# Making the context's modulation columns beside token blocks 2 and 3, and the context's tokens and states earlier in the first head pair

## The chip, the cores and the metric

The kernel runs on one core of a Trainium2 chip. The metric is the device time of one execution, in microseconds; the median of three runs is given. The engines are TensorE (PE in the profile), VectorE (DVE), ScalarE (ACT), GpSimd (POOL) and SyncE (SP, which issues most DMAs). Each engine carries out its own instructions in a fixed order and waits on semaphores for what other engines make.

## The reference

One layer of a hybrid diffusion backbone over 2048 tokens of width 1024, with 256 context tokens. What bears on the change is the modulated input of the context and the state that it leaves for the scans:

```python
mod_c = jax.nn.silu(c_ctx) @ w_mod[l] + b_mod[l]
csh1, csc1, cgt1, csh2, csc2, cgt2 = jnp.split(mod_c[None, None, :], 6, axis=-1)

uc = modulate(layer_norm(ctx), csh1, csc1)
fc, qc, kc, vc, gc = mixer_inputs(uc, w_in[l])
yc, st_f, st_b = bidirectional_retention(qc, kc, vc, lg_f, lg_b, state0, state0)

u = modulate(layer_norm(x), sh1, sc1)
f, q, k, v, g = mixer_inputs(u, w_in[l])
q = axial_rope(q, row_pos, col_pos)
k = axial_rope(k, row_pos, col_pos)
y, _, _ = bidirectional_retention(q, k, v, lg_f, lg_b, st_f, st_b)
mix = jnp.concatenate([fourier_mix(f), gated_group_norm(y, g)], axis=-1) @ w_out[l]
x = layer_norm(DEEPNORM_ALPHA * x + gt1 * mix, ln1_g[l], ln1_b[l])
```

Here `modulate(xn, shift, scale)` is `xn * (1 + scale) + shift`. The retention works in chunks of 128 tokens with one state per head and direction: each chunk adds to the state, decayed by the chunk's factor, and reads the state before it ("cross") and itself ("inner"). The latent tokens' scans start from the context's final states. A SwiGLU channel mixer follows.

## The kernel before, in words

Weights and activations are split into a high and a low f16 part, and every product of the large projections is three matmuls (lines 152 to 154, `mm3`). The 2048 tokens are four blocks of 512. The Tile scheduler sets the order of instructions on each engine from the program's text and its own timeline, so an instruction can stand far from where the text has it.

- *Blocks 0 and 1* are normalised and modulated together with the modulation's own columns: column block k (128 channels) of shift and scale is a product of `w_mod` with the conditioning vector, for the latent tokens (`smod[0]`) and, for k = 0 and 1 alone (`ON_PE = 2`), also for the context (`smod[1]`).
- *Blocks 2 and 3* follow in the loop `for b in range(2, NB)`: load four token tiles, two early projections (`early_mm`) of the first pair's q, k and v, normalise (line 229), and for each k four transposes (line 236), the f16 part on ScalarE (line 241), the f32 value on VectorE (line 246) and their difference on GpSimd (line 247). The Fourier group's projections and transforms come next, with more early projections: eight of sixteen chunks are projected when the pairs begin.
- *Three head pairs.* Each has a first pass (`first_pass`), which in every step projects a chunk and does rotation, turn (transposes), score and inner product of two ready ones, and then calls `side(s)` for work that is to lie beside it. In the first pair, `side1` starts one context column (`ctx_cols`) in each of the steps 0 to 5, the two context tiles (`ctx_tile`) in steps 5 and 6 and the context's keys and states (`pair.context()`) in step 8. Then `scans` carry the states from chunk to chunk on VectorE (`scan1`, line 684), and the second pass (`second_pass`) does gates (`gate`, SiLU at line 772), the cross products (line 784) and the normalised output. The modulation's columns of the later stages are summed in steps of the other pairs (`rest`).
- *A context column* (`ctx_cols`): `mod_sum` loads 1024 x 256 weights of `w_mod` in two tiles of 512 KB (line 559), sums them on VectorE with the vector's values, eight instructions of 128x256 (lines 561 and 563); two matmuls with a column of ones (line 572) add up the partitions; `mod_cols` (line 215) writes `smod[1][k]`. It yields after the sum, so that the matmuls come a step later.
- *A context tile* (`ctx_tile`): load (512 KB), normalise, eight transposes in two groups (line 586) and for each of them two activations of ScalarE (lines 241 and 244) and a subtraction.
- *The context's states* (`context`): two projections, keys (line 624), and four instructions that make the first state of each direction (lines 673 and 674).

All these weights and tiles go through three `raw` buffers of 512 KB, which are taken in the order of the program's text; a load waits until its buffer's last reader is done.

Of the kernel before, what the change touches and what calls it, by code (L numbers as in the profile page):

```python
# [12 lines left out]
ALU = mybir.AluOpType  # L13
PSUM = bass.MemoryType.PSUM

P = 128
D = 1024
KT = D // P
# [61 lines left out]
def layer_kernel(ctx: ExitStack, tc: tile.TileContext, a, out):  # L80
    nc = tc.nc
    V, S, G, T, Q = nc.vector, nc.scalar, nc.gpsimd, nc.tensor, nc.sync
    x_in = a["x"][0]
    ctx_in = a["ctx"][0]
    w_mod = a["w_mod"][0]
# [10 lines left out]
    def nm(s):  # L96
        uid[0] += 1
        return f"{s}_{uid[0]}"

    def mk(pool, shape, dt=F32, tag=None, bufs=1):  # L100
        return pool.tile(shape, dt, name=nm(tag), tag=tag, bufs=bufs)
# [8 lines left out]
    def const(shape, tag, dt=F32):  # L110
        return cp.tile(shape, dt, name=tag, tag=tag, bufs=1)


    pa = ctx.enter_context(tc.tile_pool(name="psum", bufs=1, space=PSUM))
# [13 lines left out]
    def raw_tile(shape=(P, 2, 512), dt=F32):  # L128
        return mk(wp, list(shape), dt, tag="raw", bufs=3)
# [6 lines left out]
    ones = const([P, 1], "ones")  # L136
# [57 lines left out]
    sil = const([P, 2, 8], "sil")  # L194
# [7 lines left out]
    def gemv(pool, raw, v, cols, tag):  # L202

        acc = mk(pool, [P, cols], tag=tag, bufs=2)
        V.tensor_scalar_mul(acc, raw[:, 0], sil[:, v, 0:1])
        for k in range(1, KT):
            V.scalar_tensor_tensor(acc, raw[:, k], sil[:, v, k : k + 1], acc, ALU.mult, ALU.add)
        return acc


    smod = [[const([P, 2], f"smod{v}_{k}") for k in range(KT)] for v in range(2)]
    smod2 = [const([P, 2], f"smod2_{k}") for k in range(KT)]

    def mod_cols(dst, pm, sub, k):
        V.scalar_tensor_tensor(dst, pm, SU, bmod[:, sub, k], ALU.mult, ALU.add)
# [15 lines left out]
    def u_part(pool, xs, hi, lo, s, k, tag, on_act):  # L231

        w = len(xs) * P
        pt = mk(pa, [P, 512], tag=tag, bufs=1)
        for i, xt in enumerate(xs):
            T.transpose(pt[:, i * P : (i + 1) * P], xt[:, k * P : (k + 1) * P], ident)
        u_split(pool, pt[:, :w], hi, lo, s, on_act)

    def u_split(pool, pt, hi, lo, s, on_act):
        w = pt.shape[1]  # L240
        S.activation(hi, pt, AF.Identity, scale=s[:, 1:2], bias=s[:, 0:1])
        u32 = mk(pool, [P, w], tag=f"u32_{w}", bufs=2)
        if on_act:
            S.activation(u32, pt, AF.Identity, scale=s[:, 1:2], bias=s[:, 0:1])
        else:
            V.tensor_scalar(u32, pt, s[:, 1:2], s[:, 0:1], ALU.mult, ALU.add)
        G.tensor_tensor(lo, u32, hi, ALU.subtract)
# [26 lines left out]
    def load_x(b):  # L274
        r = []
        for i in range(4):
            t = mk(sp, [P, D], tag="x", bufs=9)
            Q.dma_start(t, x_in[(b * 4 + i) * P : (b * 4 + i + 1) * P])
            r.append(t)
        return r  # L280

    ON_PE = 2
# [22 lines left out]
    q0, k0 = FW, FW + QKW  # L305
# [17 lines left out]
    for k in range(KT):  # L323
        while k and len(wms) < min(KT, k + 7):
            load_wm()
        pm = mk(pa, [P, 2, 2], tag="misc", bufs=2)
# [6 lines left out]
        else:  # L333
            acc = gemv(sp, wms[k].rearrange("p k i n -> p k (i n)"), 0, 2 * P, "macc")
# [24 lines left out]
    def early_mm(i):  # L359
# [4 lines left out]
            proj(ps, uhi[b][:, k, ts_], ulo[b][:, k, ts_], wq0[k], k)  # L364
        S.copy(early[i], ps)

    for b in range(2, NB):
        xs[b] = load_x(b)
        u_tiles(b)
        early_mm(2 * b - 4)  # L370
        for t in xs[b]:
            normalise(sp, t)
        early_mm(2 * b - 3)
        for k in range(KT):
            u_part(sp, xs[b], uhi[b][:, k], ulo[b][:, k], smod[0][k], k, ("tq", "zt")[k % 2], False)

    rope = ca.tile([P, NT, P], F32, name="rope", tag="rope", bufs=1)
    Q.dma_start(rope, a["rope"])
# [170 lines left out]

    gate_rows = [dram_tile([1, D], F32, f"gate{i}") for i in range(2)]  # L550


    def mod_sum(segs, v):

        r = []
        for k0 in range(0, KT, 4):
            raw = raw_tile((P, 4, 2, P))
            for i, c0 in enumerate(segs):
                Q.dma_start(raw[:, :, i], w_mod[k0 * P : (k0 + 4) * P, c0 : c0 + P].rearrange("(k p) n -> p k n", p=P))
            r.extend(raw[:, k].rearrange("p i n -> p (i n)") for k in range(4))  # L560
        V.tensor_scalar_mul(r[0], r[0], sil[:, v, 0:1])
        for k in range(1, KT):
            V.scalar_tensor_tensor(r[0], r[k], sil[:, v, k : k + 1], r[0], ALU.mult, ALU.add)
        return r[0]

    def ctx_cols(k):

        acc = mod_sum([i * D + k * P for i in range(2)], 1)
        yield
        pm = mk(pa, [P, 2], tag="zt", bufs=1)  # L570
        for i in range(2):
            T.matmul(pm[:, i : i + 1], acc[:, i * P : (i + 1) * P], ones, start=True, stop=True)
        mod_cols(smod[1][k], pm, 0, k)

    def ctx_tile(i):
        if not cu:
            cu.extend(up.tile([P, KT, CTX], F16, name=t, tag=t, bufs=1) for t in ("chi", "clo"))
        t = raw_tile((P, D))
        Q.dma_start(t, ctx_in[i * P : (i + 1) * P])
        normalise(rp, t)  # L580
        yield
        cs = slice(i * P, (i + 1) * P)
        for k0 in range(0, KT, 4):
            pt = mk(pa, [P, 4, P], tag="zt", bufs=1)
            for k in range(4):
                T.transpose(pt[:, k], t[:, (k0 + k) * P : (k0 + k + 1) * P], ident)
            for k in range(4):
                u_split(rp, pt[:, k], cu[0][:, k0 + k, cs], cu[1][:, k0 + k, cs], smod[1][k0 + k], True)
# [318 lines left out]
    def start(g):  # L907
        next(g)
        going.append(g)
# [10 lines left out]
    for p, pair in enumerate(pairs):  # L920
        wgu = pair.wg_units()

        def side1(s):
            go(s)
            if s is None:
                return
            if p == 0:
                n = KT - ON_PE
                if s < n:
                    start(ctx_cols(ON_PE + s))  # L930
                if s in (n - 1, n):
                    start(ctx_tile(s - n + 1))
                elif s == n + 2:
                    start(pair.context())
            elif s == 1:
                start(pair.context())
            if p and (p == 2 or s < 10) and rest:
                start(rest.pop(0)())
            if s >= (4 if p == 0 else 8) and wgu:
                wgu.pop(0)()  # L940

        nxt = pairs[p + 1].wq_units() if p + 1 < PAIRS else []

        def side2(s):
            go(s)
            if s is None:
                return
            if s >= 2 and s % 2 == 0 and nxt:
                nxt.pop(0)()
            elif p == PAIRS - 1 and s >= 3 and s % 2 and s < 11:  # L950
                wo_unit(0, s // 2 - 1, ws_tile)

        pair.first_pass(side1, early if p == 0 else ())
        pair.second_pass(orders[p][1], side2)
    es_r.close()
# [551 lines left out]
    for o, sb in TWO:  # L1507
        hq, last = h_next
        n = TWO.index((o, sb)) + 1
# [163 lines left out]
```

## Time and profile before

| | before |
|---|---|
| runs | 2156.97, 2154.32, 2148.89 us |
| median | 2154.32 us |
| profiled execution | 2151.64 us |
| its span | 2149.8 us |
| mean granted clock of TensorE | 0.976 |
| PE busy | 2036.8 us (95%) |
| DVE busy | 1402.3 us (65%) |
| ACT busy | 790.1 us (37%) |
| POOL busy | 761.2 us (35%) |

Busy time counts an engine's instructions, not its waits. Times in the trace are counted from the start of the span. A granted clock of 1.00 is TensorE's full clock, 0.50 half of it. A matmul's shown duration overlaps the next one's start, so the distance between two starts is what one costs.

### The profile page before, as it was taken

The page shows a single profiled execution, that of the slowest core. Times are in us where ns is not written, and L with a number is a line of the kernel's source. Part 1 is how long each engine was busy: PE and PEld are TensorE (multiplying, and loading weights), DVE is VectorE, ACT ScalarE, POOL GpSimd, SP SyncE. Part 2 cuts the span into 40 slices and gives each one's busy share as a digit, 9 for nine tenths or more (in the row PEclk, how much of TensorE's full clock was granted, in tenths as well). Part 3 has the DMA queues.
Part 4 walks back from the last instruction along what each step waited for, and adds up shares of the span by engine and source line. Part 5 has one row for each costly group of instructions (what it writes and reads, how often), then busy time and mean ns, then how long its engine had stood idle before and what let it go on. Part 6 is the DMA issues. An engine that isn't in the chain of part 4 may idle for free. (4 is left out here: it accounts for less than half of the span.)

```text
span 2149.8 us, 30986 instructions
## 1 busy us (share of the span) xinstructions
PE 2036.8 (95%) x11678; PEld 1187.4 (55%) x11678; DVE 1402.3 (65%) x2545; ACT 790.1 (37%) x1434; POOL 761.2 (35%) x804
## 2 busy tenths in 40 slices
PE   6899979999999899979899999999999899999998
PEld 5457567558557544434344444444444348888743
DVE  7865575657546577786566555655664548878776
ACT  5623532233233244443333433343334324333132
POOL 3322402121222136646665566556655400000010
PEclk8998989999999999989999999999999999999999
DMA  9602221332211445634434443444344359665752
GB/s 288 200 2 91 79 72 60 109 90 66 89 45 50 161 167 196 230 128 122 141 125 144 122 150 118 141 132 147 121 130 144 103 198 346 209 224 208 246 184 105
DMA packets 300342, 305.19 MB, mean 142 GB/s; under 512 B 15448, under 2 KB 248992, under 8 KB 299040
## 3 DMA queue, kind: packets, MB, share of 16 engines
q1 hardware_dynamic: 293376, 287.08, 41.8%
q10 hardware_dynamic: 6816, 16.12, 2.0%
q8 instruction: 92, 1.51, 0.3%
q14 instruction: 58, 0.48, 0.1%
HBM read 200.25 MB, written 102.90 MB: 141 GB/s over the span
## 5 line engine op out<-in xcount | busy, mean ns | idle before, releaser
L152 PE MATMUL proj<-ws,uhi 128*128 128x512 f16 (+1 forms) x768 | 250.9, 327 | 4.6 <-ACT sg L772 2.5
L154 PE MATMUL proj<-ws,ulo 128*128 128x512 f16 (+1 forms) x768 | 250.9, 327 | 0.0
L153 PE MATMUL proj<-ws,uhi 128*128 128x512 f16 (+1 forms) x768 | 250.7, 326 | 0.0
L153 PEld LDWEIGHTS <-ws 128*128 128x128 f16 x1296 | 128.0, 99 | 175.3 <-issue 24.8
L152 PEld LDWEIGHTS <-ws 128*128 128x128 f16 x1296 | 128.1, 99 | 156.4 <-issue 8.1
L154 PEld LDWEIGHTS <-ws 128*128 128x128 f16 x1296 | 127.6, 98 | 155.6 <-issue 6.0
L167 POOL TENSOR_TENSOR rstd<-ve,mhalf 128x1 f32<-128x1 f32 x66 | 38.0, 584 | 461.2 <-DVE ve L165 446.6
L149 DVE SCALAR_TENSOR_TENSOR ws<-raw,ws 128x512 f16<-128x512 f32 x186 | 149.9, 821 | 70.5 <-ACT ws L148 69.1
L148 ACT ACTIVATE ws<-raw 128x512 f16<-128x512 f32 x186 | 112.3, 625 | 94.9 <-DMA raw<-in_w_ffn_gate_dram 25.1
L152 PE MATMUL proj<-u2b,ws 128*128 128x512 f16 x344 | 130.2, 383 | 12.9 <-ACT b L1324 7.5
L1158 ACT CAST ho<-h 128x1280 f16<-128x1280 f32 x70 | 87.4, 1258 | 144.6 <-DVE h L1430 36.5
L149 DVE SCALAR_TENSOR_TENSOR wdo<-raw,wdo 128x256 f16<-128x256 f32 (+1 forms) x100 | 67.0, 694 | 103.6 <-ACT wdo L148 101.9
L152 PE MATMUL misc<-u2a,ws 128*128 128x512 f16 x344 | 130.2, 379 | 3.7 <-ACT b L1324 2.9
L154 PE MATMUL proj<-u2b,ws 128*128 128x512 f16 x344 | 132.1, 384 | 0.0
L153 PE MATMUL proj<-u2b,ws 128*128 128x512 f16 x344 | 132.1, 384 | 0.0
L153 PE MATMUL misc<-u2a,ws 128*128 128x512 f16 x344 | 130.4, 379 | 0.0
L154 PE MATMUL misc<-u2a,ws 128*128 128x512 f16 x344 | 130.4, 379 | 0.0
L1159 DVE TENSOR_TENSOR ho<-h,ho 128x1280 f16<-128x1280 f32 x70 | 103.9, 1488 | 21.0 <-ACT ho L1158 20.9
L153 PEld LDWEIGHTS <-uhi 128*128 128x128 f16 x768 | 75.3, 98 | 47.7 <-issue 6.6
L154 PEld LDWEIGHTS <-ulo 128*128 128x128 f16 x768 | 75.3, 98 | 45.1 <-issue 0.6
L152 PEld LDWEIGHTS <-uhi 128*128 128x128 f16 x768 | 76.0, 99 | 42.6 <-issue 1.7
L149 DVE SCALAR_TENSOR_TENSOR wdo<-ws,wdo 128x512 f16<-128x512 f32 (+2 forms) x70 | 52.8, 774 | 70.9 <-ACT wdo L148 68.5
(494 smaller groups left out, 5315.5 us busy)
## 6 DMA issues: line engine op xcount, KB each, us to landing
h<-h SPq DMA_DIRECT2D x40, 640.0 KB
raw<-in_w_mod_dram SPq DMA_DIRECT2D x88, 256.0 KB
wd<-wdo SPq DMA_DIRECT2D x50, 448.0 KB
wd<-wd SPq DMA_DIRECT2D x33, 640.0 KB
h<-sg SPq DMA_DIRECT2D x60, 256.0 KB
raw<-in_w_ffn_gate_dram SPq DMA_DIRECT2D x22, 512.0 KB
raw<-in_w_ffn_up_dram SPq DMA_DIRECT2D x22, 512.0 KB
raw<-in_w_ffn_down_dram SPq DMA_DIRECT2D x40, 256.0 KB
```

Source lines behind the costliest of these rows:

```text
L148: S.activation(hi, raw, AF.Copy, scale=scale)
L149: V.scalar_tensor_tensor(lo, raw, scale, hi, ALU.mult, ALU.subtract)
L152: T.matmul(o, sh, mh, start=first, stop=False, skip_group_check=onto)
L153: T.matmul(o, sh, ml, start=False, stop=False, skip_group_check=onto)
L154: T.matmul(o, sl, mh, start=False, stop=last, skip_group_check=onto)
L167: pows.append(G.tensor_tensor(rstd, ve, mhalf[:, 0:n], ALU.pow).ins)
L1158: S.copy(dst[:, 0], src)
L1159: V.tensor_tensor(dst[:, 1], src, dst[:, 0], ALU.subtract)
```

## The change

The functions `mod_sum` and `ctx_cols` move up, ahead of the loop over blocks 2 and 3. `ctx_cols` no longer yields between sum and matmuls, and its PSUM tile has the tag `misc` (two buffers) where it had `zt` (one). In the loop, after the column blocks k = 1, 4 and 7 of each of the two blocks, one context column is made (six in all, k = 2 to 7 of the context). In the first pair the two context tiles start in steps 1 and 2 (were 5 and 6), the context's states in step 4 (was 8).

```diff
+    ctx_k = list(range(ON_PE, KT))
     for b in range(2, NB):
...
         for k in range(KT):
             u_part(sp, xs[b], uhi[b][:, k], ulo[b][:, k], smod[0][k], k, ("tq", "zt")[k % 2], False)
+            if k % 3 == 1 and ctx_k:
+                ctx_cols(ctx_k.pop(0))
...
     def ctx_cols(k):

         acc = mod_sum([i * D + k * P for i in range(2)], 1)
-        yield
-        pm = mk(pa, [P, 2], tag="zt", bufs=1)
+        pm = mk(pa, [P, 2], tag="misc", bufs=2)
...
             if p == 0:
-                n = KT - ON_PE
-                if s < n:
-                    start(ctx_cols(ON_PE + s))
-                if s in (n - 1, n):
-                    start(ctx_tile(s - n + 1))
-                elif s == n + 2:
+                if s in (1, 2):
+                    start(ctx_tile(s - 1))
+                elif s == 4:
                     start(pair.context())
```

Behind the change the same lines have other numbers: the column's loads, sums and matmuls are lines 373, 375, 377 and 385, the states 675 and 676, the scans 686, the context's transposes 588, the SiLU 774 and the cross products 786.

*First place: blocks 2 and 3, TensorE and SyncE.* In the changed kernel's order on TensorE a column's two matmuls (line 385, out of the sum `raw_907`) stand between the transposes of a token block (`zt_880`, line 236) and the matmuls of a Fourier projection (`proj_1257`):

```order
L236 MATMUL zt_880<-ident,x_695 128x128
L153 LDWEIGHTS ws_330
L153 MATMUL proj_1257<-ulo_698,ws_330 128x512
L154 LDWEIGHTS ws_330
L154 MATMUL proj_1257<-uhi_697,ws_330 128x512
L152 LDWEIGHTS ws_330
L152 MATMUL proj_1257<-uhi_697,ws_330 128x512
L385 MATMUL misc_921<-ones,raw_907 128x1 x2
```

On SyncE the loads up to the Fourier constants (`cht`, `pos`) were these before, the `raw` tiles being halves of context columns:

```order
L278 DMA x_877<-in_x_dram 128x1024
L559 DMA raw_1791<-in_w_mod_dram 128x4x128 x2
L559 DMA raw_1907<-in_w_mod_dram 128x4x128 x2
L559 DMA raw_1910<-in_w_mod_dram 128x4x128 x2
L559 DMA raw_2026<-in_w_mod_dram 128x4x128 x2
L441 DMA cht_1145<-in_cht_dram 128x512
L443 DMA pos_1147<-in_pos_dram 128x4096
```

And these with the change, where `raw_1999` and `raw_2156` are the context tiles and `raw_2441` is a gate weight:

```order
L373 DMA raw_910<-in_w_mod_dram 128x4x128 x2
L373 DMA raw_1053<-in_w_mod_dram 128x4x128 x2
L373 DMA raw_1056<-in_w_mod_dram 128x4x128 x2
L373 DMA raw_1098<-in_w_mod_dram 128x4x128 x2
L373 DMA raw_1101<-in_w_mod_dram 128x4x128 x2
L373 DMA raw_1143<-in_w_mod_dram 128x4x128 x2
L373 DMA raw_1146<-in_w_mod_dram 128x4x128 x2
L581 DMA raw_1999<-in_ctx_dram 128x1024
L581 DMA raw_2156<-in_ctx_dram 128x1024
L256 DMA raw_2441<-in_w_in_dram 128x2x256
L465 DMA cht_1253<-in_cht_dram 128x512
L467 DMA pos_1255<-in_pos_dram 128x4096
```

All six pairs of column matmuls now stand in this stage on TensorE, where there was none, and all six sums on VectorE, where three stood before; the Fourier constants moved behind the loads of every column, both context tiles and a gate weight.

*Second place: the last context keys and the states, TensorE and VectorE.* Before, the last keys of the context (`misc_2788`) stood on TensorE in the third gate (`proj_2881`):

```order
L154 LDWEIGHTS ulo_880
L154 MATMUL proj_2881<-ws_2420,ulo_880 128x256
L624 MATMUL misc_2788<-y_2784,kz_2786 128x128 x2
L152 LDWEIGHTS uhi_879
L152 MATMUL proj_2881<-ws_2420,uhi_879 128x256
```

With the change they are `misc_2689` and stand in the first gate (`proj_2825`), before two scores of a late chunk:

```order
L152 MATMUL proj_2825<-ws_2699,uhi_933 128x256
L762 MATMUL misc_2682<-vt_2598,sT_2660 128x128 x2
L626 MATMUL misc_2689<-y_2579,kz_2687 128x128 x2
L755 MATMUL s_608_2737<-qkT_2719 128x128
L755 MATMUL s_609_2740<-qkT_2719 128x128
L153 LDWEIGHTS uhi_933
L153 MATMUL proj_2825<-ws_2699,uhi_933 128x256
```

On VectorE the states and the first scans before, with sums of a gate's modulation (`raw_3587`, `raw_3698`) between them:

```order
L673 SCALAR_TENSOR_TENSOR kvs_337_1753<-y_2757,gch,misc_2788 64x128
L674 SCALAR_TENSOR_TENSOR kvs_587_2615<-misc_2788,gch,y_2757 64x128
L563 SCALAR_TENSOR_TENSOR raw_3587<-raw_3590,sil,raw_3587 128x256
L684 SCALAR_TENSOR_TENSOR kvs_327_1723<-kvs_337_1753,gch,kvs_327_1723 64x128
L561 TENSOR_SCALAR raw_3698<-raw_3698,sil 128x256
L684 SCALAR_TENSOR_TENSOR kvs_550_2488<-kvs_587_2615,gch,kvs_550_2488 64x128
```

And with the change:

```order
L675 SCALAR_TENSOR_TENSOR kvs_355_1861<-y_2552,gch,misc_2689 64x128
L676 SCALAR_TENSOR_TENSOR kvs_598_2693<-misc_2689,gch,y_2552 64x128
L756 SCALAR_TENSOR_TENSOR sT_2736<-s_608_2737,dT 128x128
L618 TENSOR_TENSOR kz_2779<-qk_2761,ze 128x256
L756 SCALAR_TENSOR_TENSOR sT_2736<-s_609_2740,dT 128x128
L377 SCALAR_TENSOR_TENSOR raw_3587<-raw_3587,sil 128x256
L686 SCALAR_TENSOR_TENSOR kvs_345_1831<-kvs_355_1861,gch,kvs_345_1831 64x128 x2
```

The keys moved from the third gate to the first. All 60 scan steps still stand behind the states in both orders; from the last keys to the first cross product TensorE now has 190 gate matmuls instead of 159, and on VectorE 52 of the scan steps and 14 instructions of sums stand between the states and the last scan step that the first cross product reads, the other eight and three more sums behind it.

## Rows read from the trace of the kernel before

**Rows 1.** The page's busy time by engine and its forty slices of the span

```profile
PE 2036.8 (95%) x11678; PEld 1187.4 (55%) x11678; DVE 1402.3 (65%) x2545; ACT 790.1 (37%) x1434; POOL 761.2 (35%) x804
...
PE   6899979999999899979899999999999899999998
```

**Rows 2.** Windows, us: length, busy time of each engine, TensorE clock, DMA share, GB/s

```profile
86.00:130.00 44.00, 41.82 (x217) 21.83 (x215) 21.93 (x45) 19.49 (x31) 19.97 (x19) 1.00 0.24 78
...
189.90:218.50 28.60, 24.33 (x134) 20.12 (x133) 20.12 (x60) 13.96 (x37) 15.30 (x22) 0.76 0.36 102
198.00:211.60 13.60, 13.60 (x53) 11.33 (x53) 9.82 (x32) 5.79 (x16) 6.10 (x9) 0.50 0.27 78
...
303.00:325.00 22.00, 8.11 (x39) 7.32 (x37) 17.17 (x51) 1.90 (x4) 2.00 (x2) 0.61 0.09 24
```

**Rows 3.** Timeline of PE around the first cross products: start, duration, instruction

```profile
285.28 0.61 PE L624 MATMUL misc<-y,kz 128*128 128x128 f32 x4
...
302.97 0.27 PE L154 MATMUL proj<-ws,ulo 128*128 128x256 f16 x1
315.68 3.76 PE L784 MATMUL misc<-kvs,qxT 128*128 128x128 f32 x16 [12.43 <-DVE kvs L684]
...
324.65 0.27 PE L152 MATMUL proj<-ws,uhi 128*128 128x256 f16 x1 [0.52 <-ACT sg L772]
...
330.76 1.06 PE L784 MATMUL misc<-kvs,qxT 128*128 128x128 f32 x8
331.65 0.27 PE L152 MATMUL proj<-ws,uhi 128*128 128x256 f16 x1
```

**Rows 4.** Timeline of VectorE: the first state, a run of scans, the last

```profile
286.61 0.33 DVE L673 SCALAR_TENSOR_TENSOR kvs<-y,gch,misc 64x128 f32<-64x128 f32 x1
...
303.88 4.89 DVE L684 SCALAR_TENSOR_TENSOR kvs<-kvs,gch,kvs 64x128 f32<-64x128 f32 x13
...
314.80 1.87 DVE L684 SCALAR_TENSOR_TENSOR kvs<-kvs,gch,kvs 64x128 f32<-64x128 f32 x5
```

**Rows 5.** Timeline of PE in the small-operation stage

```profile
189.89 0.50 PE L572 MATMUL zt<-ones,raw 128*128 128x1 f32 x4
190.25 0.31 PE L735 MATMUL tq<-ident,qk 128*128 128x128 f32 x1
...
196.11 0.49 PE L760 MATMUL misc<-vt,sT 128*128 128x128 f32 x2 [1.74 <-DVE sT L754]
```

**Rows 6.** Timeline of VectorE beside blocks 2 and 3

```profile
101.19 0.35 DVE L561 TENSOR_SCALAR raw<-raw,sil 128x256 f32<-128x256 f32 x1 [4.05 <-DMA raw<-in_w_mod_dram]
...
101.98 0.81 DVE L246 TENSOR_SCALAR u<-tq,smod 128x512 f32<-128x512 f32 x1
```

**Rows 7.** Timeline of PE beside blocks 2 and 3

```profile
102.84 0.66 PE L236 MATMUL tq<-ident,x 128*128 128x128 f32 x4 [0.61 <-DVE u L246]
```

**Rows 8.** Timeline of SyncE: the first Fourier constant's issue

```profile
98.13 0.50 SPq L441 DMA_DIRECT2D cht<-in_cht_dram  x1
```

**Rows 9.** Timeline of PE: the first cosine matmuls

```profile
144.52 0.59 PE L508 MATMUL misc<-cht,fR 128*128 128x256 f32 x2
```

**Rows 10.** Timeline of ScalarE: normalisation, the context's activations, a table load

```profile
83.64 2.37 ACT L229 ACTIVATE x<-x,nmr,rstd 128x1024 f32<-128x1024 f32 x2
...
265.35 0.46 ACT L241 ACTIVATE chi<-zt,smod 128x128 f16<-128x128 f32 x1 [1.63 <-PE zt L586]
265.70 0.45 ACT L244 ACTIVATE u<-zt,smod 128x128 f32<-128x128 f32 x1
...
279.95 1.28 ACT L772 ACT_TABLE_LOAD   x1
```

**Rows 11.** Timeline of PE: a group of the context's transposes, and what follows

```profile
249.03 0.60 PE L586 MATMUL zt<-ident,raw 128*128 128x128 f32 x4
249.47 0.61 PE L760 MATMUL misc<-vt,sT 128*128 128x128 f32 x4
```

**Rows 12.** Timeline of VectorE in the small-operation stage

```profile
195.97 0.75 DVE L563 SCALAR_TENSOR_TENSOR raw<-raw,sil,raw 128x256 f32<-128x256 f32 x1
```

More of the change, by code (lines that the diff above doesn't have):

```diff
@@ L365, in early_mm, with mod_sum, ctx_cols @@
         S.copy(early[i], ps)
+    def mod_sum(segs, v):
+        r = []
+        for k0 in range(0, KT, 4):
+            raw = raw_tile((P, 4, 2, P))
+            for i, c0 in enumerate(segs):
+                Q.dma_start(raw[:, :, i], w_mod[k0 * P : (k0 + 4) * P, c0 : c0 + P].rearrange("(k p) n -> p k n", p=P))
+            r.extend(raw[:, k].rearrange("p i n -> p (i n)") for k in range(4))
+        V.tensor_scalar_mul(r[0], r[0], sil[:, v, 0:1])
+        for k in range(1, KT):
+            V.scalar_tensor_tensor(r[0], r[k], sil[:, v, k : k + 1], r[0], ALU.mult, ALU.add)
+        return r[0]
+    def ctx_cols(k):
+        acc = mod_sum([i * D + k * P for i in range(2)], 1)
+        pm = mk(pa, [P, 2], tag="misc", bufs=2)
+        for i in range(2):
+            T.matmul(pm[:, i : i + 1], acc[:, i * P : (i + 1) * P], ones, start=True, stop=True)
+        mod_cols(smod[1][k], pm, 0, k)
+    ctx_k = list(range(ON_PE, KT))
     for b in range(2, NB):
@@ L550, in layer_kernel @@
     gate_rows = [dram_tile([1, D], F32, f"gate{i}") for i in range(2)]
[L553 to L568, printed above, removed]
-        yield
-        pm = mk(pa, [P, 2], tag="zt", bufs=1)
-        for i in range(2):
-            T.matmul(pm[:, i : i + 1], acc[:, i * P : (i + 1) * P], ones, start=True, stop=True)
-        mod_cols(smod[1][k], pm, 0, k)
     def ctx_tile(i):
```

## Prediction

> **What bounds the kernel now.** I began with the page's shares: TensorE is busy for 2036.8 of 2149.8 us, and of the forty slices only the first two, the sixth (269 to 322 us), three in the middle and the last stand under nine tenths [rows 1]. So a change of order can only give back what TensorE loses there, and I cut the first 325 us into the stages that the change touches [rows 2]. Beside the normalisation of blocks 2 and 3 (86 to 130 us) PE is idle for 44.00 − 41.82 = 2.2 us. In the small-operation stage of the first pair (189.9 to 218.5 us: eight tiles already projected, so only rotations, turns, scores and inner products) it is idle for 28.60 − 24.33 = 4.3 us, and for 13.60 us of it the granted clock is 0.50, the lower of its two levels (1.2 GHz), where full is 2.4 GHz. At 303 to 325 us PE is busy for 8.11 of 22.00 us, at clock 0.61.
>
> PE's timeline shows the last from end to end [rows 3]. The last gate matmul starts at 302.97 and PE stops at 303.24; the first eight cross products (16 records, 3.76 us) wait 12.43 us, to 315.68, for a scanned state that VectorE makes; eight more follow, and the next gate starts at 324.65. At full clock eight records take 0.89 us (330.76 to 331.65), so the work between is 32 records, 3.56 us, and the **loss is 324.65 − 303.24 − 3.56 = 17.85 us**. VectorE's timeline shows why [rows 4]: the two directions' states from the context, four instructions, start at 286.61, right behind the last context keys (PE, 285.28), and 60 scan steps follow one after another (thirteen in 4.89 us, 0.376 each), with 15 instructions of the gates' modulation sums among them, until 314.80 + 1.87 = 316.67. That is 30.06 us; 64 × 0.376 = 24.06 leave 0.40 for each of the 15. VectorE has no gap there, so only the start or its other work can move the end.
>
> **The change, part by part.** Sums are against the profiled execution's 2151.64 us, which stands 2.7 below the median of 2154.32.
>
> *A, blocks 2 and 3.* The order shows that the scheduler had already put three of the six column sums here; what comes is three more sums (3 × 8 × 0.40 = 9.6 us of VectorE, busy 21.93 of 44 now [rows 2], so hidden) and all six pairs of column matmuls on PE. A pair takes 190.25 − 189.89 = 0.36 us [rows 5]: 2.2 us. Each is placed by hand, so PE, in order, waits there for VectorE's sum, and VectorE for the load: a load whose buffer VectorE had just freed landed 4.05 us later [rows 6]. Before, VectorE alone stood in that wait, and PE felt 0.61 us of it through the modulated tokens [rows 7]. If the pairs fall into PE's 2.2 us of idle time, the stage costs 0; if each of five hand-overs adds one modulation operation of VectorE (0.81 [rows 6]), 2.2 + 4.1 = 6.3. I take the pairs' own time and the waits as they were: **+2** (0 to +6). On SP the loads of the later columns, of both context tiles and of a gate weight go ahead of the Fourier constants, which before were issued from 98.13 on [rows 8]; now they wait for the last column pair, ahead of the stage's last transposes. Even from the stage's end, 130, there are 14 us to the first cosine matmul at 144.52 [rows 9], so I put this at nothing; a landing later than that would be paid in full.
>
> The Trainium skill (DMA: Bandwidth & Descriptors, Anatomy of one DMA) fits a DMA by 2.0 us plus its bytes over 436 GB/s. By that an estimate for 512 KB is 3.2 us against the row's 4.05, each hand-over would be 0.85 us shorter, and the sum below would be some 2 us lower.
>
> *B, the small-operation stage.* It loses the sums of three columns on VectorE (19 records in the trace, about 8 us of 20.12) and their four pairs of matmuls (three of 0.36 and one, at half clock, near 0.8). It gains both context tiles: their normalisation on ScalarE (2.37 us for two [rows 10]) and three of four groups of transposes with 24 of 32 activations (0.345 each, 265.35 to 265.70 [rows 10]): 8.3 us. ScalarE goes from 13.96 to about 24.6 of 28.6 us [rows 2]: it fits, barely. On PE three groups of transposes (0.44, 249.03 to 249.47 [rows 11]) replace the four pairs: −0.6. Waits for a score's mask product (1.74 us at 196.11 [rows 5]) get shorter without a sum of 0.4 to 0.75 us queued ahead on VectorE [rows 12]. **−1.** Upper bound: the three groups at half clock (0.88 each) and one more wait of 1.74, less what goes: +4. Lower: the clock never falls, 13.6 / 2 = 6.8, and the waits go: −8.
>
> *C, to the second pass* (218.5 to 303). Three groups of transposes (0.44) and two column pairs (0.36) are no longer here: **−2** (−3 to 0).
>
> *D, the scan stall.* The last context keys move from the third gate into the first, so 190 gate matmuls instead of 159 stand between them and the first cross product, with four small groups (scores, a turn, keys, inner products). A gate matmul takes (302.97 − 285.28 − 0.44) / 158 = 0.109 us [rows 3], a small group about 0.4 (a column pair 0.36, a group of transposes 0.44 [rows 5, 11]); PE's way from the keys to the first cross is 0.4 + 190 × 0.109 + 1.6 = 22.8 us. VectorE's from the keys to the state it needs: 1.3 (285.28 to 286.61) + 56 states and scans × 0.376 + 14 instructions of sums × 0.40 + 1.3 for four masks and a product kz (0.2 to 0.4 apiece as an estimate from the 0.376 of a scan) = 29.3; to its last scan 8 × 0.376 + 3 × 0.40 = 4.2 more, 33.5. So the scans are still late. PE waits 6.5 us, does eight cross products and ten gate matmuls (1.1), waits for VectorE's two sums y behind its last scan (33.5 + 0.8 = 34.3), does the other eight (1.8 at full, 3.76 at half clock) and goes on 0.52 later [rows 3], at 36.6 to 38.6. Its work to there is 22.8 + 3.56 + 1.1 = 27.5, so the loss is 9.1 to 11.1; I take 10.0, **−7.8**. Bounds: 9.1 with the clock up, −8.8; and with a modulation load late by 4.05 among the scans (VectorE is in order), −3.8. Two more table loads stand on ScalarE here (1.28 us each [rows 10]); they lie beside gates whose banks are free again before PE needs them, and cost up to 2.6 if they don't.
>
> Sum: 2 − 1 − 2 − 7.8 = −8.8, **2142.8, given as 2143.0 us**: the stall halves, and the rest about cancels.
>
> **Rivals.**
> 1. *The clock stays up in the small-operation stage.* The fall to 0.50 in 198 to 211.6 comes behind the 1.74 us wait at 196.11. VectorE's sums lie right before the late masks (0.75 us at 195.97 [rows 12]); without them the wait may vanish and the stage lose only the −6.8 of the half clock more: 2142.8 − 6.8 + 1 = 2137. Against it: ScalarE is at 24.6 of 28.6 us there.
> 2. *New waits there.* PE's small operations now also wait for ScalarE to empty the bank of each group of transposes (eight activations, 2.8 us), and the stage stays at half clock to its end: B at its upper bound, 2142.8 + 1 + 4 = 2148. For: those 24.6 us. Against: the groups share no bank with the scores.
> The Trainium skill (TensorE: Matmul & The Clock Gate, HAM oscillation — how this bites in real kernels) says that bursts of matmuls with waits between them fall back to the low clock again and again. The stretch at 0.50 behind the wait at 196.11 agrees with it; by the rule this rival is worth more than the first.
> 3. *The stall stays.* If PE stands at the context keys for VectorE's kz, which waits for ScalarE's copy out of the last context projection, the states start no earlier and D is nothing: 2151.64 + 2 − 1 − 2 = 2151. It decides from 7.8 us of wait there. For: ScalarE is nearly full just before. Against: the order puts two further projections and sixteen gate matmuls between that projection and the keys.
> 4. *Slower: the load and the pairs chase each other in blocks 2 and 3.* With three load buffers, a load waits for PE's pair (release), PE for VectorE's sum, VectorE for the load. Each of five hand-overs could then cost its whole 4.05 us on PE: 20.3 us, 2142.8 + 20.3 = 2163. It decides where a landing takes over about 6 us, the 4.05 plus the 2 us by which the placing leads. For: the loads stand on SP one behind the other, so a late release holds up all that follow. Against: the queue moves only 78 GB/s on the mean of this stage [rows 2], and the one row that shows a landing [rows 6].
>
> **How the numbers follow.** The forecast gets 0.47, the rivals 0.18, 0.10, 0.14 and 0.11. About 0.5%, 10.8 us, is what a measurement of this kernel can tell from no change. Faster, below 2140.9, lie the first rival and about a third of the forecast, whose own bounds run from 2135 (A, C and D at their lower ends, −4.0, and B half-way, −3.5) to 2153 (A and C and D at their upper ones, +10): 0.18 + 0.17 = 0.35. Slower is nearly all of the fourth rival, 0.10; the rest, 0.55, is within. The range goes from 2132 (the first rival, with A, C and D at their lower ends: 2137 − 4.0 = 2133.0, and a little more) to 2156 (A and D at their upper ends, +8, and B at its, +5: 2155.8); the fourth rival and a little of the other tail are left out.
>
> **What would show it.** Right: the wait of the first cross falls from 12.4 to some 6.5 us, PE's loss before the gate that follows to about 10, scans ending about 33 us behind the context keys; six pairs of 0.36 us before 130 us, and the stage's end within 2 us of now; the half-clock stretch still there. Wrong: waits of PE on column sums of several us each; a wait at the last context keys; the stretch at 0.50 gone; Fourier matmuls waiting on their constants.

## The result, and the profile after

| | before | changed |
|---|---|---|
| median | 2151.51 us (5 runs, the three above among them) | 2140.20 us (2139.36 to 2140.80, 5 runs) |
| profiled execution's span | 2149.8 us | 2137.5 us |
| mean granted clock of TensorE | 0.976 | 0.981 |
| PE busy | 2036.8 us | 2029.4 us |

The ratio is 0.9944, 95% interval 0.9930 to 0.9959: 11.3 us or 0.56% less. The page of the changed kernel, busy time and forty slices (answers to [rows 1]):

```profile
PE 2029.4 (95%) x11678; PEld 1180.2 (55%) x11678; DVE 1404.2 (66%) x2545; ACT 792.0 (37%) x1436; POOL 764.3 (36%) x804
...
PE   6899989999999899979999999999999889999998
```

The sixth slice has gone from 7 to 8, and nothing else that the change touches shows at this scale. The timeline of TensorE in the changed kernel gives the marks (start, duration, instruction; in brackets a wait and its releaser):

```profile
61.40 0.64 PE L236 MATMUL tq<-ident,x 128*128 128x128 f32 x4
...
135.40 0.38 PE L152 MATMUL proj<-ws,uhi 128*128 128x512 f16 x1 [0.25 <-ACT fT L318]
...
194.58 0.27 PE L737 MATMUL tq<-ident,qk 128*128 128x128 f32 x1
...
274.60 0.61 PE L626 MATMUL misc<-y,kz 128*128 128x128 f32 x4
...
301.21 0.27 PE L153 MATMUL proj<-ws,uhi 128*128 128x256 f16 x1
303.90 3.45 PE L786 MATMUL misc<-kvs,qxT 128*128 128x128 f32 x16 [2.42 <-DVE kvs L686]
...
308.86 2.02 PE L786 MATMUL misc<-kvs,qxT 128*128 128x128 f32 x16 [0.41 <-DVE y L788]
313.13 0.27 PE L152 MATMUL proj<-ws,uhi 128*128 128x256 f16 x1 [2.25 <-ACT sg L774]
...
314.04 0.42 PE L153 MATMUL proj<-ws,uhi 128*128 128x256 f16 x1
...
320.91 1.06 PE L786 MATMUL misc<-kvs,qxT 128*128 128x128 f32 x8
```

Two of these marks in the kernel before, for the first stage:

```profile
61.38 0.64 PE L236 MATMUL tq<-ident,x 128*128 128x128 f32 x4
...
130.71 0.38 PE L152 MATMUL proj<-ws,uhi 128*128 128x512 f16 x1 [0.25 <-ACT fT L318]
```

Read between marks, up to the third pair of cross products (330.76 before [rows 3], 320.91 now, 9.85 us sooner):

- *Blocks 2 and 3*, from the first transposes to the last Fourier projections: 69.33 us before, 74.00 now, **+4.7**.
- *The Fourier stretch*, 130.71 to the first turn at 190.25 [rows 5]: 59.54, now 59.18, −0.4.
- *The first pass*, from that turn to TensorE's stop at the cross products: 190.25 to 303.24, 112.99; now 194.58 to 301.48, 106.90. Ten gate matmuls (1.09) have moved behind the stop, so **−5.0**.
- *The stall*: 303.24 to 324.65, of which 17.85 were lost; now 301.48 to 313.13, less 3.56 of cross products and 1.09 of gates, 7.0 lost, **−10.85**.
- *Behind it* the gates run at half clock for a while (0.21 apart at 314.04, where 0.109 is full clock): +1.7.

These sum to −9.85. The rest of the span is 2.4 us shorter, though neither code nor order differ much there; in the fourteen profiles of this case (these two and the twelve below) it lies anywhere from 1815.3 to 1823.9 us, so I put the 2.4 down to nothing.

### The profile page after: what moved, and what is told of

Read it like the earlier page. It is cut to its first block, busy times and chain, and to the rows that moved or that the text cites. A ratio compares the mean times of both kernels' runs of the same rounds, so it can differ in the third digit from the quotient of the medians.

```text
span 2137.5 us, 30994 instructions
## 1 busy us (share of the span) xinstructions
PE 2029.4 (95%) x11678; PEld 1180.2 (55%) x11678; DVE 1404.2 (66%) x2545; ACT 792.0 (37%) x1436; POOL 764.3 (36%) x804
```

## The experiments

The first four ask which part of the change the time comes from.

**Columns alone.** The context's tiles and states back at their old steps:

```diff
-                if s in (1, 2):
-                    start(ctx_tile(s - 1))
-                elif s == 4:
+                if s in (5, 6):
+                    start(ctx_tile(s - 5))
+                elif s == 8:
                     start(pair.context())
```

> The columns stay beside blocks 2 and 3; the context's tiles go back to steps 5 and 6 and its states to step 8. Theory (the gain comes from the earlier states, and the columns' move costs): the first stages stay some 4.7 us late, and the wait of the first cross product is back above 8 us (2.4 in the changed kernel), so the time is 2149 to 2155 us, no better than before. Rival (the gain comes from taking the sums out of the first pass, whenever the states are made): the first pass keeps what it won and the time stays within 3 us of the changed kernel's 2140.

Measured: 2151.84 us, ratio to before 0.9999 (0.9989 to 1.0009). The waits of TensorE, 90 to 340 us (us in total, times, longest):

```profile
PE misc L786 <- DVE kvs L686: 11.1, 1, 11.1
PE tq L236 <- DVE u L246: 3.3, 4, 1.4
```

The theory holds: moving the columns alone gains nothing, the stall is back. The rival has a part, though: from the first turn to TensorE's stop the pass takes 109.84 us (195.83 to 305.67) where it took 112.99, so 3.2 of the 5.0 us stay won. They only pay for part of blocks 2 and 3, which take 74.99 us here.

**States in step 6.**

```diff
-                elif s == 4:
+                elif s == 6:
```

> Only the states' step is changed, from 4 to 6, halfway back to 8. Theory (the step of the states sets the stall): the last context keys come later on TensorE, the wait of the first cross product grows from 2.4 to between 6 and 12 us, 2144 to 2150 us. Rival (the scans end when VectorE has done its other work, whatever the step): the same wait within 1 us and 2139 to 2142 us.

Measured: 2150.62 us, ratio 0.9991 (0.9979 to 1.0004), the wait 11.6 us. The wait is as the theory said, the time a little above its range: halfway back in steps is all the way back in time. Since the tiles stay in steps 1 and 2 here, their earlier steps alone gain nothing either. The last context keys come at 283.27, 8.7 us later than in the changed kernel, and the scans come in another order, which lengthens the wait too and of which more below.

**States in step 3.**

```diff
-                elif s == 4:
+                elif s == 3:
```

> Only the states' step is changed, from 4 to 3. Theory (the step of the states sets the stall): the scans start about a step sooner, the wait of the first cross product goes, and of the changed kernel's 7 us between its last gate and the next some 5 to 6 are won: 2133 to 2136 us. Rival (scans then stand on VectorE before rotations and score masks of the last chunks, and TensorE waits for those): waits for masks grow by 4 us or more, 2139 to 2144 us.

Measured: 2137.57 us, ratio 0.9930 (0.9915 to 0.9945). Between the two ranges, and its interval overlaps the changed kernel's (0.9930 to 0.9959), so a gain over step 4 isn't shown by the time. The timeline of TensorE shows the mechanism of the theory:

```profile
294.36 2.02 PE L786 MATMUL misc<-kvs,qxT 128*128 128x128 f32 x16 [0.70 <-DVE kvs L686]
...
300.20 1.13 PE L786 MATMUL misc<-kvs,qxT 128*128 128x128 f32 x8 [0.33 <-DVE y L788]
```

The scan wait went from 2.42 to 0.70 us, while the waits for masks that the rival feared did not come (1.2 us in all from 190 to 345, where the changed kernel has 3.4). Its profiled execution, though, lost 2.1 us against the changed kernel's in blocks 2 and 3 (76.14 against 74.00 by the marks above), where the two have the same code: that stage scatters.

**Sums cut short** in the six columns (six of eight terms left out, all loads kept):

```diff
-        acc = mod_sum([i * D + k * P for i in range(2)], 1)
+        acc = mod_sum([i * D + k * P for i in range(2)], 1, True)
...
-        for k in range(1, KT):
+        for k in range(4, KT, 4) if short else range(1, KT):
```

> Left out: six of the eight terms of each context column's sum (all loads stay), so VectorE has 36 instructions of 0.40 us fewer, most of them beside blocks 2 and 3. Theory (the stage of blocks 2 and 3 became 4.7 us longer because the modulated tokens queue behind the sums on VectorE): its end comes back to within 2 us of 130.7, and the time is 2135 to 2138 us. Rival (the loads' landing behind their buffers' release holds the sums and through them TensorE): the stage still ends at 134 us or later, 2139 to 2142 us.

Measured: 2143.18 us, ratio 0.9957 (0.9942 to 0.9971). Blocks 2 and 3 take 72.71 us (61.97 to 134.68), 3.4 more than before, and end past 134 as the rival said; the time is a little above the rival's range. Cutting the sums does not bring the stage back. TensorE's waits there (us in total, times, longest) say what took their place:

```profile
PE misc L385 <- issue: 2.1, 1, 2.1
PE misc L385 <- DVE raw L377: 2.0, 2, 1.5
PE misc L385 <- PE proj L152: 0.6, 1, 0.6
PE zt L236 <- DVE u L246: 0.4, 1, 0.4
```

In the changed kernel the transposes wait 3.8 us for modulated tokens (`u`) and the pairs 1.8 us for their sums:

```profile
PE tq L236 <- DVE u L246: 3.2, 4, 1.2
PE misc L385 <- DVE raw L377: 1.8, 2, 1.2
PE zt L236 <- DVE u L246: 0.6, 1, 0.6
```

Without the sums the wait for tokens is nearly gone, and TensorE stands at the pairs instead, 4.7 us in all. The third cross products came at 318.75, 2.2 sooner than in the changed kernel; the rest of the span is 7.3 us longer, where its trace shows no single wait, and I leave that open.

The next five ask where the columns belong.

**Columns in the Fourier stretch.**

```diff
-            if k % 3 == 1 and ctx_k:
-                ctx_cols(ctx_k.pop(0))
...
             early_mm(i)
+            for _ in range(1 + i % 2):
+                ctx_cols(ctx_k.pop(0))
```

> The six columns are written beside the Fourier group's early projections (one or two behind each of the last four) and no longer in blocks 2 and 3; tiles in steps 1 and 2 and states in step 4 as in the changed kernel. Theory (blocks 2 and 3 became longer because VectorE waits for column loads with modulated tokens behind it): from the first transposes at 61.4 us to the last Fourier projections' start it is 69 to 71 us again (69.3 before, 74.0 in the changed kernel), and the time is 2134 to 2137 us. Rival (a column costs the same wherever it is made, since in the Fourier stretch the transform's additions stand behind the loads on VectorE): the first turn of the first pair comes within 1.5 us of the changed kernel's 194.6, and the time is 2139 to 2142 us.

Measured: 2148.39 us, ratio 0.9981 (0.9968 to 0.9993). Blocks 2 and 3 are back at 68.36 us (60.98 to 129.34), as the theory said. The rival's sign came true as well: the first turn comes at 194.87, within 0.3 us of the changed kernel's, since the Fourier stretch now takes 65.53 us where it took 59.18:

```profile
129.34 0.38 PE L152 MATMUL proj<-ws,uhi 128*128 128x512 f16 x1 [0.25 <-ACT fT L318]
...
194.87 0.33 PE L737 MATMUL tq<-ident,qk 128*128 128x128 f32 x1 [2.26 <-POOL qk L731]
```

So the six columns cost about as much there as in blocks 2 and 3. The time is far above both ranges, for a reason that neither named. In its windows (length; busy PE, PEld, DVE, ACT, POOL; clock; DMA share; GB/s) and in VectorE's timeline:

```profile
190.00:200.00 10.00, 3.95 (x22) 2.24 (x20) 5.75 (x16) 2.09 (x6) 2.00 (x4) 0.86 0.65 229
```

```profile
197.70 1.29 DVE L178 BATCH_NORM_STATS2 st<-raw 128x6 f32<-128x512 f32 x2 [2.96 <-DMA raw<-in_ctx_dram]
```

The context tiles' loads stand behind the last columns in the same three buffers. They now land in the middle of the small operations, VectorE waits for them in order, and so does TensorE for the product `kz` that VectorE makes behind them:

```profile
200.27 1.19 PE L626 MATMUL misc<-vt,kz 128*128 128x128 f32 x4 [2.10 <-DVE ve L165]
```

From the first turn to the first projection behind the small operations it is 31.00 us (194.87 to 225.87), where the changed kernel has 25.47. Where the changed kernel's early columns pay 4.7 us, they also buy that the tiles are there in time.

**The same, states in step 3.** On top of the last edit:

```diff
-                elif s == 4:
+                elif s == 3:
```

> As the kernel before it, with the context's states in step 3. Theory (the two gains are of different stages and add): 2131 to 2135 us, faster than both. Rival (the first pass then has the tiles' activations, the states and the scans at once, and its waits eat the gain): within 1.5 us of the kernel with step 4 in the same call, or above it.

Measured: 2146.50 us, ratio 0.9970 (0.9957 to 0.9983), 1.9 below the kernel with step 4: neither its range nor clearly the rival's. The late tiles cost more than the step can give.

**Weights from the first blocks' buffers.** Two of the columns' weights are in the chip already, the others are loaded a whole column ahead:

```diff
-        acc = mod_sum([i * D + k * P for i in range(2)], 1)
+        if k in (2, 7):
+            raw = wms[k]
+        else:
+            raw = mk(sp, [P, KT, 2, P], tag="wm", bufs=3)
...
+        acc = gemv(sp, raw.rearrange("p k i n -> p k (i n)"), 1, 2 * P, "macc")
...
-    ctx_k = list(range(ON_PE, KT))
+    ctx_k = [2, 7, 3, 4, 5, 6]
```

> Same six columns beside blocks 2 and 3, same sums and pairs, but their weights come from the three larger buffers of the first blocks' modulation weights: two columns (k = 2 and 7) are there already and are not loaded again, the other four are loaded a column ahead. Theory (what made blocks 2 and 3 longer is VectorE waiting for a load with modulated tokens behind it, not the sums or the pairs): waits of VectorE for column loads fall from 7.2 us to under 2, the stage from the first transposes to the last Fourier projections shrinks from 74.0 to 70 to 72 us, and the time is 2134 to 2138 us. Rival (the sums' own time on VectorE and the pairs on TensorE make it): it stays at 73 us or more, 2139 to 2142 us.

Measured: 2137.70 us, ratio 0.9942 (0.9930 to 0.9954). VectorE waits for no column load any more (6.5 and 1.4 us from 60 to 136 in the changed kernel), and the stage still takes 73.04 us:

```profile
63.21 0.64 PE L236 MATMUL tq<-ident,x 128*128 128x128 f32 x4
...
136.25 0.38 PE L152 MATMUL proj<-ws,uhi 128*128 128x512 f16 x1 [0.25 <-ACT fT L318]
```

By the stage the rival is right, so the loads' landing is not the main part of it either: the transposes still wait 3.1 us for modulated tokens. The median falls in the theory's range, but the ratio is the changed kernel's (0.9944) within 0.0002, so no gain is shown.

**The same, states in step 3.**

```diff
-                elif s == 4:
+                elif s == 3:
```

> As the kernel before it, with the context's states in step 3. Theory (the gains are of different stages and add): 2 to 4 us below the kernel with step 4 of the same call, 2130 to 2135 us, the fastest of all. Rival (in the first pass the earlier states cost TensorE as much in waits for VectorE and ScalarE as they save at the cross products): within 1.5 us of the kernel with step 4, or above it.

Measured: 2136.03 us (2132.56 to 2136.95), ratio 0.9932 (0.9919 to 0.9946), 1.7 below the same kernel with step 4 (2137.70): between theory and rival. It has the lowest median here of the kernels that compute everything, but its ratio is no lower than that of step 3 alone (0.9930), so it isn't shown to be faster than that.

**Four columns and two**, states in step 3:

```diff
-            if k % 3 == 1 and ctx_k:
+            if k in (1, 4) and ctx_k:
                 ctx_cols(ctx_k.pop(0))
...
             early_mm(i)
+            if i == 4:
+                ctx_cols(ctx_k.pop(0))
+                ctx_cols(ctx_k.pop(0))
```

> Four columns beside blocks 2 and 3 (behind k = 1 and 4), two behind the first of the Fourier group's last four early projections, states in step 3. Theory (each column beside blocks 2 and 3 costs about a sixth of the 4.7 us, and two columns are hidden in the Fourier stretch as long as their tiles' loads come in time): 2134 to 2136 us, 1 to 3 below the same step with all six columns there (2137.6). Rival (the context tiles' loads, behind the last columns in the same three buffers, come late as with six columns in that stretch): the stage of the small operations gets longer, 2138 to 2146 us.

Measured: 2140.41 us, ratio 0.9950 (0.9937 to 0.9963). The stage is 73.35 us with four columns (63.25 to 136.60), not two thirds of the way to six, and the Fourier stretch with the other two is 60.08, 0.9 longer. The time falls in the rival's range, and the small operations, from the first turn to the first projection, do take longer (196.68 to 224.09, 27.41 us, against 25.50 with step 3 alone), but VectorE waits for no load among them: the rival's reason is not what the trace shows.

The last three ask what makes the scans' chain as long as it is.

**Short gate sums.** In the changed kernel, six of eight terms of the gate rows' sums left out, loads kept:

```diff
-        acc = mod_sum((c0, c0 + P), 0)
+        acc = mod_sum((c0, c0 + P), 0, True)
```

> Left out, in the changed kernel: six of the eight terms of each sum for the gate rows (loads stay), so that two or three instead of 17 instructions of sums stand among the scans. Theory (the scans end as late as the work between them makes them): the last scan ends some 5 to 6 us sooner behind the states, the wait of the first cross product (2.4 us) goes, and the time is 2133 to 2137 us. Rival (what then bounds the gates' restart is the chain from the cross product to the freed gate buffers, which waited 2.25 us): the last gate before and the next after the cross products stay at least 5 us of lost time apart, and the time is 2138 to 2141 us.

Measured: 2136.00 us, ratio 0.9923 (0.9907 to 0.9939): the theory's range. From the first state to the end of the last scan it is 25.7 us instead of 29.3, less of a gain than the theory's 5 to 6, since VectorE waits 1.4 us for loads in it. The wait of the first cross product is 1.21 us, and TensorE is busy for 9.95 of the 10 us from 300 to 310, where it was for 7.17 in the changed kernel. VectorE's timeline of this kernel gave a number that I had not looked for:

```profile
288.32 2.17 DVE L686 SCALAR_TENSOR_TENSOR kvs<-kvs,gch,kvs 64x128 f32<-64x128 f32 x8
290.43 0.27 DVE L756 SCALAR_TENSOR_TENSOR sT<-s,dT 128x128 f32<-128x128 f32 x1
```

By the program's order (the trace itself doesn't name the direction) these eight scans are all of the forward direction (partitions 0 to 63). They take 2.11 / 8 = 0.264 us each; in the kernel with the columns alone, forward and backward steps (partitions 64 to 127) alternate one by one:

```profile
293.49 4.51 DVE L686 SCALAR_TENSOR_TENSOR kvs<-kvs,gch,kvs 64x128 f32<-64x128 f32 x12
```

That is 0.376 each, as before the change [rows 4]. In the changed kernel they come two forward, two backward, thirteen in 4.21 us, 0.32 each (the starts are 0.27 and 0.38 us apart by turns):

```profile
278.64 0.33 DVE L675 SCALAR_TENSOR_TENSOR kvs<-y,gch,misc 64x128 f32<-64x128 f32 x1
...
298.25 4.21 DVE L686 SCALAR_TENSOR_TENSOR kvs<-kvs,gch,kvs 64x128 f32<-64x128 f32 x13
...
306.78 1.16 DVE L686 SCALAR_TENSOR_TENSOR kvs<-kvs,gch,kvs 64x128 f32<-64x128 f32 x4
```

**The kernel before, states by direction**, to see whether that is a matter of order alone:

```diff
                 V.scalar_tensor_tensor(self.slot(0)[0:64, hs], c0[0:64, hs], gc[0:64], kvc[1][0:64, hs], ALU.mult, ALU.add)
+            for h in range(2):
+                hs = slice(h * P, (h + 1) * P)
+                gc = gch[:, 2 * p + h : 2 * p + h + 1]
                 V.scalar_tensor_tensor(self.slot(NT - 1)[64:128, hs], kvc[1][64:128, hs], gc[64:128], c0[64:128, hs], ALU.mult, ALU.add)
```

> The kernel before, with one edit: the four instructions that make the context's states are written both heads of the forward direction first, then both of the backward one, so that VectorE's 60 scan steps come as two forward, two backward, where they came one forward, one backward; steps, columns and their places are those of before. Theory (a scan step on the other 64 partitions than the instruction ahead of it costs 0.376 us, one on the same partitions 0.264): the mean spacing of scan steps falls to about 0.32, the chain from the first state to the last scan from 30.06 to 26 to 27 us, the wait of the first cross product from 12.4 to 9 us, and the time is 3 to 4 us below before. Rival (the shorter spacing belongs to the later place in the program, other loads or other neighbours): the chain stays at 29.5 to 30.5 us and the time within 1.5 us of before.

Measured: 2150.00 us, ratio 0.9998 (0.9987 to 1.0008). Its timelines of VectorE and of TensorE:

```profile
297.39 4.23 DVE L687 SCALAR_TENSOR_TENSOR kvs<-kvs,gch,kvs 64x128 f32<-64x128 f32 x13
```

```profile
308.67 3.75 PE L787 MATMUL misc<-kvs,qxT 128*128 128x128 f32 x16 [11.06 <-DVE kvs L687]
```

The spacing is the theory's: thirteen in 4.23 instead of 4.89 us, at the old place in the program, so it goes with the order. The chain is shorter by less than it said, 28.67 us (280.76 to 309.43), since VectorE waited 1.23 us for a modulation load in it and a sum ahead of a scan now took 0.5 us (293.51 to 294.01) instead of 0.4. The cross products' wait fell by 1.4 us instead of 3.4, and the time is in the rival's range: the order alone gains nothing that the time can show.

**The kernel with the lowest median, states by direction.** The same edit there:

```diff
+            for h in range(2):
+                hs = slice(h * P, (h + 1) * P)
+                gc = gch[:, 2 * p + h : 2 * p + h + 1]
                 V.scalar_tensor_tensor(self.slot(NT - 1)[64:128, hs], kvc[1][64:128, hs], gc[64:128], c0[64:128, hs], ALU.mult, ALU.add)
```

> The fastest kernel so far (column weights from the larger buffers, states in step 3), with the same edit of the states' order. Theory (its scans already come in pairs of one direction in the first head pair, and TensorE no longer waits for a scan there): within 2 us of it, 2134 to 2138 us. Rival (the second and third pair's scans, still one forward, one backward, hold TensorE too): 3 us or more below it, under 2133.

Measured: 2136.22 us, ratio 0.9938 (0.9920 to 0.9956): as the theory said, nothing to be had where TensorE doesn't wait for scans.

## Why the prediction was right, and where its steps were not

The forecast was 8.8 us less by sum, and 11.3 were measured; the first rival's 2137 and the no-change case at 2151 lie on either side. That the sum came so near is in part luck: the marks above show 9.85 us won, with A 2.7 us worse than forecast and B, C and D together 3.8 better, and the other 2.4 us by which the profiled execution is shorter lie behind them. Two readings of the rows were slightly off and bear on nothing: four slices in the middle, not three, stand under nine tenths, and VectorE has one gap of 0.17 us among the scans (at 297.74). The forecast's terms, by their own names:

**A, blocks 2 and 3: +2 predicted, +4.7 measured; this term was mis-sized.** The step that failed is "the pairs' own time and the waits as they were". The pairs took 0.36 to 0.47 us each, 2.4 in all, as forecast; the waits of TensorE for modulated tokens grew from 1.1 to 3.8 us, and with them the stage's end moved by 4.7 us instead of the 2 that were to be the sign of being right. VectorE's timeline and, at the same place, TensorE's in the changed kernel:

```profile
99.25 0.48 DVE L377 SCALAR_TENSOR_TENSOR raw<-raw,sil,raw 128x256 f32<-128x256 f32 x1 [3.03 <-DMA raw<-in_w_mod_dram]
99.65 0.81 DVE L246 TENSOR_SCALAR u<-tq,smod 128x512 f32<-128x512 f32 x1
```

```profile
100.51 0.66 PE L236 MATMUL tq<-ident,x 128*128 128x128 f32 x4 [1.21 <-DVE u L246]
```

VectorE waits 3.03 us for a column's load with the modulation of a token block next in its order, and the transposes wait 1.21 us for that. I had this chain (as an upper bound and as the fourth rival) and took it at zero. The experiments say how much of it is what: with the six columns here the stage takes 74.0 to 76.1 us in five kernels of the same code for it, with no pairs there (the kernel before among them) 68.2 to 70.2, with the sums cut 72.7, with the loads' waits gone 73.0. So neither sums nor loads alone carry the cost; either taken away gives back 1 to 3 us. With the sums cut the tokens no longer wait and the pairs do; with the loads' waits gone the tokens still wait behind the sums. The pairs' own time and the places that the order gives them remain; a kernel with the pairs alone was not run, and how the rest divides stays open. The fourth rival was wrong in size: TensorE waited for column sums twice, 1.8 us in all. The Fourier constants, issued some 32 us later (130.25 instead of 98.13), were waited for by nobody, as the step said. The fit of a DMA that the prediction set beside the 4.05 us is given by the Trainium skill (DMA: Bandwidth & Descriptors, Anatomy of one DMA) for the GpSimd path, while SyncE issues these loads; and as A held no hand-over, the sum could not have come out 2 us lower by it.

**B and C, −3 predicted together, −5.0 measured (−5.4 with the pair): B was mis-sized.** In the windows of the changed kernel:

```profile
200.00:210.00 10.00, 6.37 (x32) 4.30 (x30) 6.83 (x16) 9.54 (x27) 7.79 (x13) 0.73 0.11 32
210.00:220.00 10.00, 8.56 (x53) 7.42 (x54) 7.91 (x22) 9.30 (x26) 8.85 (x15) 0.76 0.33 101
220.00:301.50 81.50, 79.90 (x544) 54.08 (x543) 42.60 (x123) 33.01 (x78) 18.31 (x29) 1.00 0.19 54
```

ScalarE is full in the first two (9.54 and 9.30 of 10), TensorE waits, and the half-clock stretch is still there, some 5 us in each, about ten where there were 13.6. The first projection behind the small operations divides B from C, before and now:

```profile
218.50 0.38 PE L152 MATMUL proj<-ws,uhi 128*128 128x512 f16 x1 [1.04 <-ACT vt L721]
```

```profile
203.69 0.49 PE L755 MATMUL s<-qkT 64*128 64x128 f32 x4 [1.19 <-ACT qkT L741]
...
220.05 0.38 PE L152 MATMUL proj<-ws,uhi 128*128 128x512 f16 x1
```

From the first turn to it the stage takes 28.25 us before and 25.47 now, −2.8, and with the pair that stood ahead of that turn (the −0.4 above) B is −3.1 where −1 was forecast. Some 0.9 of it is only moved: eight matmul records of scores and inner products now stand behind that projection. The half-clock stretch, about 3.4 us shorter, gave back some 1.7 that the forecast did not have. The first rival (clock up) fell, and so did the second: new waits of ScalarE came (1.2 us for its copies and 1.1 for a bank of transposes), but the stage got shorter. The Trainium skill (TensorE: Matmul & The Clock Gate, HAM oscillation — how this bites in real kernels) says that waits between bursts bring the low clock back; the trace agrees in that the half clock lies right behind waits of 0.54, 0.42 and 1.19 us (200.69 to 203.69), though the 1.21 us at 100.51 left it at 1.00, and the sum that it favoured, 2148, was not reached. C, from that projection to the stop, is 84.74 us before and 81.43 with 1.09 of gates behind the stop now, −2.2, near the −2 forecast (−3.1 without the eight records that came in). From 220 on the clock is 1.00 throughout and TensorE idle for 1.6 us, where the stretch from 218.5 had 2.2 idle and 0.98:

```profile
218.50:303.00 84.50, 82.33 (x564) 58.13 (x563) 48.78 (x132) 40.11 (x98) 23.62 (x41) 0.98 0.30 86
```

That small operations spread among projections also wait less without the tiles' work was not in my sum.

**D, the stall: −7.8 predicted, −10.85 measured, 1.7 given back as half clock; right in mechanism, its parts mis-sized.** The last scan ends 33.3 us behind the context keys (274.60 to 307.94), as forecast (33.5), but out of other parts: the states start 4.0 us behind the keys instead of 1.3, VectorE having other work then, and the chain from there takes 29.3 instead of 32.2, because scans in pairs cost 0.32 and not 0.376 (60 × 0.056 = 3.4 us, less 0.8 for a load that VectorE waited for). The wait of the first cross product was to be 6.5 and is 2.42: TensorE came later, 26.9 us behind the keys instead of 22.8, for the most part since there were seven small groups where I counted four, and 1.4 us of waits. Behind the cross products it is the gates' buffer that is late (2.25 us instead of the 0.52 of before). The third rival, the stall stays, is what the first two experiments made by hand, with the states in steps 8 and 6 (step 5 was not run); here the keys were not held up.

So the states' step carries the gain (step 8: 11.1 us of wait and no gain; step 6: 11.6 and none; step 4: 2.4; step 3: 0.7), and the columns' early place is what that step is paid with. The scheduler gave the scans their cheaper order with steps 4 and 3 and the dearer one with 8 and 6, so some 3.4 us of the wait's fall, by the estimate above, go with the order; by the order alone the kernel before won 1.4 us of wait and no time.

## What to carry to other kernels

A chain of dependent steps on an engine that is off the critical path most of the time bounds the program at the one place where the matmuls need its end; look for where it can start, and count what the earlier start costs elsewhere. Of a load placed early, ask what stands behind its first reader on that engine: here a modulated token waited on VectorE for a weight that nobody needed yet. And a buffer ring passes lateness on: six columns made later cost as much where they went, and made the context tiles late, which cost another 5.5 us.

## What the hardware showed that was not expected

- A VectorE step on 64 partitions x 128 elements costs 0.264 us behind one on the same 64 partitions and 0.376 us behind one on the other 64; one forward, one backward is the dearest order of the two scans that was seen. Nearly all scan steps that follow each other directly are 0.26 to 0.27 or 0.36 to 0.39 us apart in the traces of this case, and where the order of the states alone was changed, the spacing went with it; that the partitions and not some other difference between the directions make it was not tried.
- The same early stage with the same code took 74.0 to 76.1 us in five kernels' profiles, a scatter as large as some of the gains sought here.
